# New home addresses for the tiles in SBUF, and down projections that take high and low input parts in one 512-column matmul

## The chip, the cores and the metric

The kernel runs on one core of a Trainium2 chip. The metric is the device time of one execution in microseconds (us), as the median of several runs. The engines are called as the profile calls them: PE (TensorE matmuls), PEld (TensorE weight loads), DVE (VectorE), ACT (ScalarE), POOL (GpSimd) and SP (SyncE, which issues DMAs).

## The reference, cut to what matters

The reference sends 256 tokens of width 1,024 through one block with a mixer (two attentions), a squared-ReLU MLP and a gated per-layer embedding (PLE), and then through two layers of a second block, each with a SwiGLU, a mixer and another SwiGLU. All data are float32.

```python
# first block
x = x + einsum(merged, w_o)                     # mixer
u = relu(einsum(rmsnorm(x, g_mlp), w_up))       # 1024 -> 4096
x = x + einsum(u * u, w_down)                   # 4096 -> 1024
x = x + sigmoid(einsum(rmsnorm(x, g_ple), w_ple_gate)) * einsum(p, w_ple)
# second block, twice
x = x + 0.5 * swiglu(rmsnorm(x, g[0]), ffn_w_in[0], ffn_w_out[0])   # 1024 -> 2 * 2816, 2816 -> 1024
x = x + mixer(rmsnorm(x, g[1]))                 # GLA and forgetting attention, then sparse attention
x = x + 0.5 * swiglu(rmsnorm(x, g[2]), ffn_w_in[1], ffn_w_out[1])
```

## The kernel before

**Layout.** Activations lie with features on the 128 partitions and the 256 tokens along the free dimension: a tile `[128, 8, 256]` is the whole residual `x`. Weights come in one long stream of DMAs of 512 KB, in the order in which they are used (class `Stream`). Each such chunk of 128x1024 lands in `wraw`, ACT casts it to `whi` (the high part, type float32r), and DVE subtracts to get `wlo`, the low part (lines 140 and 149). There are five `wraw`, five `whi` and four `wlo` buffers, of 4,096 bytes a partition each.

**Matmuls.** Every input of a projection is also kept as a high and a low part (`hx` and `lx` for the normalised residual, `gh` and `gl` for the hidden layer, `oh` and `ol` for attention outputs, `mh` and `ml` for the merged mixer). One product of a 128x128 weight piece with a 128x256 input takes three matmuls, with the weights stationary (helper `mm3`, lines 313 to 315):

```python
PE.matmul(o, ah, bh, start=start, stop=False, ...)   # L313: whi x hx
PE.matmul(o, ah, bl, start=False, stop=False, ...)   # L314: whi x lx
PE.matmul(o, al, bh, start=False, stop=stop_, ...)   # L315: wlo x hx
```

Each of the three loads its own 128x128 weights. `gemm_a` walks the output tiles of 128 features in pairs that share one PSUM bank (`acc`, three buffers), and inside a tile over the K inputs. `gemm_b` does the opposite for values and for the last projection: the input is stationary and the weights move, in 256 or 512 columns (lines 363 to 365).

**The stages around the change.** The stages follow each other in program order: mixer, MLP up, MLP down (`w_down`: 8 output tiles, K = 32), PLE, and four SwiGLUs called ffn00, ffn01, ffn10 and ffn11 with a mixer after ffn00 and after ffn10. The down projections of ffn00, ffn01 and ffn10 have 8 output tiles and K = 22; that of ffn11 goes through `gemm_b`. At the end of each pair of output tiles, `ev_down` (L935) or `ev` (L1078) scales the bank by a row, adds it to `x` (L462), and `feed` makes the next stage's `hx` and `lx` (L390, L391) and the squares for its norm (L453, L456, L457). The next stage begins with `lead=6`: two pairs of output tiles take inputs 0 to 5 first, so that inputs 6 and 7 are wanted last. The order of the work on each engine is the order in which the program emits it (a hand-written scheduler, `Sched`).

**Addresses.** A pool lays out its tiles one after the other in each partition, and pools follow each other: constants, `raw`, `hl` (`whi` and `wlo`), `act` (`x`, `hx`, `lx` of 8,192 bytes each, then two `ssq` of 2,048), `tmp` (buffers of 2,048 and 1,024 bytes), `tiny` (7 names of 6 buffers of 64 bytes, 2,688 bytes in all), and then the pool of the current phase. A second stack grows from the top downwards: `pe` with `pt_`, `ph` and `pl`, and under it `hx2` and `lx2`, the inputs of ffn00. A piece of weights starts at a multiple of 512 bytes in its buffer, save in the few chunks that hold a narrow piece, and an input k starts at a multiple of 1,024 bytes in its tile. The pool `raw` starts at byte 21,248, which is 83 times 256.

Of the kernel before, what the change touches and what calls it, by code (L numbers as in the profile page):

```python
# [104 lines left out]
class Stream:  # L105
# [112 lines left out]
def build(ctx, tc, nc, aps, total, stop=None):  # L218
# [3 lines left out]
    raw_pool = pool("raw", RB)  # L222
    hi_pool = pool("hl", HB)
# [19 lines left out]
    hx = act.tile([P, KD, T], F32R, name="hx")  # L243
    lx = act.tile([P, KD, T], F32R, name="lx")
# [67 lines left out]
    def mm3(o, ah, al, bh, bl, start, stop_, joint=False):  # L312
        PE.matmul(o, ah, bh, start=start, stop=False, skip_group_check=joint)  # L313
        PE.matmul(o, ah, bl, start=False, stop=False, skip_group_check=joint)  # L314
        PE.matmul(o, al, bh, start=False, stop=stop_, skip_group_check=joint)  # L315
# [66 lines left out]
    def rhs_of(h, l):  # L382
        return lambda k: (h[:, k], l[:, k])
# [80 lines left out]
    hrhs = rhs_of(hx, lx)  # L464
# [11 lines left out]
    def idx(a, n):  # L476
        return list(range(a, a + n))
# [39 lines left out]
    oh = mpo.tile([P, 8, T], F32R, name="oh")  # L517
    ol = mpo.tile([P, 8, T], F32R, name="ol")
# [34 lines left out]
    ckh = mp.tile([P, T], F32R, name="ckh")  # L553
    ckl = mp.tile([P, T], F32R, name="ckl")
    cqh = mp.tile([P, 2, T], F32R, name="cqh")
    cql = mp.tile([P, 2, T], F32R, name="cql")
# [23 lines left out]
    def ckv_side(c, sq):  # L580
# [12 lines left out]
        split(ckh, ckl, cn)  # L593
# [30 lines left out]
    def tok_scale(ms, n, out, const):  # L624
        """out = tok * rsqrt(tok^2 * ms + eps) * const for ms [P, 2, n]"""
# [248 lines left out]
    mh = mp.tile([P, 8, T], F32R, name="mh")  # L874
    ml = mp.tile([P, 8, T], F32R, name="ml")

    def gemm_merge():
        for i in range(4):
            pss = []
            for wn, k0 in (("w_oa", 0), ("w_ob", 4)):  # L880
                ps = accb()
                pss.append(ps)
                for j in range(2):
                    for k in range(4):
                        wh, wl = W.get((wn, k, idx((2 * i + j) * 128, 128)), P)
                        mm3(ps[:, j * T:(j + 1) * T], wh, wl, oh[:, k0 + k], ol[:, k0 + k], k == 0, k == 3)
# [16 lines left out]
    sc.run(gemm_a(8, 8, sq_cols("w_o"), rhs_of(mh, ml), lambda i, ps: sc.push(lambda: ev_wo(i, ps)), lead=6))  # L903
# [21 lines left out]
    ph = mpp.tile([P, 2, T], F32R, name="ph")  # L925
    pl = mpp.tile([P, 2, T], F32R, name="pl")
# [104 lines left out]
    sc.run(gemm_a(8, 2, sq_cols("w_ple"), rhs_of(ph, pl), ev_ple))  # L1031
# [5 lines left out]
    def ffn(layer, j, rhs, nrm, nxt):  # L1037
        mx, mp = phase("ffn%d%d" % (layer, j))
        gh = mp.tile([P, 22, T], F32R, name="gh")
        gl = mp.tile([P, 22, T], F32R, name="gl")  # L1040
# [30 lines left out]
        if nxt is None:  # L1071
            final(wout, rhs_of(gh, gl), nrm, tok, gfin, xg)
# [161 lines left out]
    def even(nrm, nxt):  # L1234
# [29 lines left out]
        oh = mp.tile([P, 8, T], F32R, name="oh2")  # L1264
        ol = mp.tile([P, 8, T], F32R, name="ol2")
# [228 lines left out]
        sc.run(gemm_a(8, 8, sq_cols("even_w_out"), rhs_of(oh, ol), lambda i, ps: sc.push(lambda: ev_o(i, ps)), lead=(4, 6),  # L1494
# [4 lines left out]
    def odd(nrm, nxt):  # L1499
# [11 lines left out]
        ch = mp.tile([P, 2, T], F32R, name="ch")  # L1511
        cl = mp.tile([P, 2, T], F32R, name="cl")
# [6 lines left out]
        oh = mp.tile([P, 8, T], F32R, name="oh3")  # L1519
        ol = mp.tile([P, 8, T], F32R, name="ol3")  # L1520
# [113 lines left out]
        crhs = rhs_of(ch, cl)  # L1634
# [52 lines left out]
        sc.run(gemm_a(8, 8, sq_cols("odd_w_out"), rhs_of(oh, ol), lambda i, ps: sc.push(lambda: ev_o(i, ps)), lead=4, width=3,  # L1687
# [8 lines left out]
    ffn(0, 0, rhs_of(hx2, lx2), n4, r5)  # L1696
# [96 lines left out]
```

## Time and profile before

| what | value |
|---|---|
| time, median of 3 runs | 1421.72 us (1413.07 to 1423.33) |
| span of the profiled execution, first to last instruction | 1410.7 us |
| PE busy, share of the span | 99% |
| PEld busy | 96% |
| DVE busy, ACT busy | 64%, 49% |
| moved from and to memory, mean | 173 GB/s |

The profile has one execution. Of its own time the profile gives the span; the median of the runs is 11.0 us above the span, the fastest run 2.4 us. Busy time of PE overstates it: a matmul of 256 columns is shown with 280 ns, while the next one starts 0.12 us after it. What a stage costs is therefore read from how many matmuls start in a stretch.

### The profile page before, as it was taken

What the parts mean: (1) busy time and instruction counts of PE and PEld (TensorE: products, weight loads), DVE (VectorE), ACT (ScalarE), POOL (GpSimd) and SP (SyncE); (2) the same over time, 40 slices, a digit from 0 to 9 for tenths busy, and PEclk for the clock granted to TensorE, in tenths of its full rate; (3) what the DMA queues carried; (4) which work ended last, traced back from release to release, by engine and by line L of the source; (5) the groups of instructions that cost most, each with busy time, mean ns of one, the idle gap of its engine ahead of it and who ended that gap; (6) DMA issues with size and microseconds to landing.
All of it is one profiled execution on the core that took longest, in us unless ns stands there. A gap on an engine that the chain in (4) does not pass through costs nothing.

```text
span 1410.7 us, 27027 instructions
## 1 busy us (share of the span) xinstructions
PE 1395.5 (99%) x11278; PEld 1360.4 (96%) x11278; DVE 903.1 (64%) x1241; ACT 685.2 (49%) x959; POOL 102.9 (7%) x108
## 2 busy tenths in 40 slices
PE   8999999999999999999999999999999999999998
PEld 8799999999999999997999999999999988999987
DVE  6766776655577656575765555655555776776553
ACT  6554465544554444453454444444444454644442
POOL 2300000000050000010000000000000171000001
PEclk9999999999999999999999999999999999999999
DMA  8633555555556565653455555555655632555652
GB/s 274 208 102 107 184 191 186 182 189 182 180 165 200 188 184 176 197 168 104 131 183 180 179 180 190 185 184 186 183 182 188 199 120 66 182 190 191 182 177 82
DMA packets 69641, 243.59 MB, mean 173 GB/s; under 512 B 7877, under 2 KB 11365, under 8 KB 69392
## 3 DMA queue, kind: packets, MB, share of 16 engines
q1 hardware_dynamic: 66096, 234.52, 52.2%
q10 hardware_dynamic: 2992, 5.99, 1.3%
q8 instruction: 88, 1.44, 0.4%
q0 software_dynamic: 432, 1.37, 0.3%
q14 instruction: 33, 0.27, 0.1%
HBM read 240.78 MB, written 4.22 MB: 174 GB/s over the span
## 4 chain that ended last, share of the span: by engine, by line
PE 95%; DVE 2%; ACT 1%; POOL 1%; issue 0%; DMA 0%; SPq 0%; POOLq 0%; DVEq 0%; ACTq 0%
PE acc L313 27%; PE acc L314 27%; PE acc L315 27%; PE acc L363 2%; PE acc L365 2%; PE acc L364 2%; PE pv L791 1%; DVE iacc L1588 1%; PE wk L760 1%; PE wk L1181 1%; PE wk L779 0%; PE wk L1660 0%; POOL rs_y L395 0%; PE wk L757 0%; PE wk L1659 0%
## 5 line engine op out<-in xcount | busy, mean ns | idle before, releaser
L149 DVE TENSOR_TENSOR wlo<-wraw,whi 128x1024 fp32r<-128x1024 f32 (+2 forms) x442 | 535.3, 1219 | 274.5 <-PE acc L315 213.0
L140 ACT CAST whi<-wraw 128x1024 fp32r<-128x1024 f32 (+1 forms) x448 | 463.5, 1039 | 396.5 <-PE acc L314 292.3
L313 PE MATMUL acc<-hx,whi 128*128 128x256 f32 x2184 | 629.1, 288 | 1.0 <-ACT whi L140 0.6
L314 PE MATMUL acc<-lx,whi 128*128 128x256 f32 x2184 | 617.1, 283 | 1.4 <-DVE lx L391 1.4
L315 PE MATMUL acc<-hx,wlo 128*128 128x256 f32 x2184 | 617.2, 283 | 0.5 <-DVE wlo L149 0.5
L313 PEld LDWEIGHTS acc<-hx,whi 128*128 128x128 f32 x2184 | 417.0, 191 | 8.3 <-issue 6.3
L314 PEld LDWEIGHTS acc<-lx,whi 128*128 128x128 f32 x2184 | 417.1, 191 | 1.9 <-DVE lx L391 1.6
L315 PEld LDWEIGHTS acc<-hx,wlo 128*128 128x128 f32 x2184 | 416.8, 191 | 0.9 <-DVE wlo L149 0.9
L314 PE MATMUL acc<-gl,whi 128*128 128x256 f32 x784 | 220.7, 281 | 0.0
L313 PE MATMUL acc<-gh,whi 128*128 128x256 f32 x784 | 220.7, 281 | 0.0
L315 PE MATMUL acc<-gh,wlo 128*128 128x256 f32 x784 | 220.7, 281 | 0.0
L313 PEld LDWEIGHTS acc<-gh,whi 128*128 128x128 f32 x784 | 147.6, 188 | 0.0
L314 PEld LDWEIGHTS acc<-gl,whi 128*128 128x128 f32 x784 | 147.6, 188 | 0.0
L315 PEld LDWEIGHTS acc<-gh,wlo 128*128 128x128 f32 x784 | 147.6, 188 | 0.0
L395 POOL TENSOR_TENSOR rs_y<-col,mhalf 128x2 f32<-128x2 f32 (+2 forms) x17 | 19.1, 1125 | 812.3 <-DVE col L423 747.9
L387 DVE TENSOR_TENSOR gl<-t,gh 128x512 fp32r<-128x512 f32 x60 | 41.6, 693 | 41.3 <-ACT gh L386 41.3
L386 ACT CAST gh<-t 128x512 fp32r<-128x512 f32 x60 | 37.2, 621 | 45.7 <-DVE t L1059 33.3
L390 ACT ACTIVATE hx<-x,gains 128x256 fp32r<-128x256 f32 x64 | 29.5, 502 | 56.9 <-DVE x L462 50.0
L313 PE MATMUL acc<-oh,whi 128*128 128x256 f32 x192 | 54.8, 286 | 0.0
L315 PE MATMUL acc<-oh,wlo 128*128 128x256 f32 x192 | 53.7, 280 | 0.0
L314 PE MATMUL acc<-ol,whi 128*128 128x256 f32 x192 | 53.7, 279 | 0.0
L1059 DVE TENSOR_TENSOR t<-t,acc 128x512 f32<-128x512 f32 x44 | 30.3, 688 | 32.4 <-ACT t L1057 32.4
(367 smaller groups left out, 1449.4 us busy)
## 6 DMA issues: line engine op xcount, KB each, us to landing
wraw<-w SPq DMA_DIRECT2D x439, 512.0 KB, 4.1
t5r<-t5u ACTq DMA_DIRECT2D x1, 3072.0 KB, 13.4
Bt<-t5r ACTq DMA_DIRECT2D x1, 2048.0 KB, 10.9
wraw<-w SPq DMA_DIRECT2D x7, 256.0 KB, 5.2
x<-xt SPq DMA_DIRECT2D x8, 128.0 KB, 4.9
rope<-cst SPq DMA_DIRECT2D x1, 640.0 KB, 7.7
gfin<-gfin POOLq DMA_DIRECT2D x1, 512.0 KB, 4.9
out<-xg ACTq DMA_DIRECT2D x2, 256.0 KB, 2.8
```

Of the source, the lines that this page charges most:

```text
L140: self.nc.scalar.copy(self.hi[c][:, :n], self.raw[c][:, :n])
L149: self.low_eng.tensor_tensor(self.lo[c][:, :n], self.raw[c][:, :n], self.hi[c][:, :n].bitcast(F32), op=OP.subtract)
L313: PE.matmul(o, ah, bh, start=start, stop=False, skip_group_check=joint)
L314: PE.matmul(o, ah, bl, start=False, stop=False, skip_group_check=joint)
L315: PE.matmul(o, al, bh, start=False, stop=stop_, skip_group_check=joint)
L363: PE.matmul(o[b][:, :N], xh[:, s], w[0], start=(k == 0), stop=False)
L364: PE.matmul(o[b][:, :N], xl[:, s], w[0], start=False, stop=False)
L365: PE.matmul(o[b][:, :N], xh[:, s], w[1], start=False, stop=(k == K - 1))
L386: S_.copy(hi, src)
L387: V.tensor_tensor(lo, src, hi.bitcast(F32), op=OP.subtract)
L390: S_.activation(hi, src, AF.Copy, scale=g)
L1059: V.tensor_tensor(u, s, ps, op=OP.mult)
```

## The change

Tiles move to other addresses, the two parts of every input come to lie side by side in one tile, and the down projections of the MLP, ffn00, ffn01 and ffn10 use a new loop.

- Unused pad tiles are laid between the pools: 64 bytes ahead of `hl`, 192 behind it, 128 behind `tiny`, 192 behind `oh` in the first mixer, 224 in the pool `pe`.
- `halves_of` makes one tile with the high part of input k, then its low part, then input k+1. `past` leaves out some 4-byte elements at its start: 32 for the MLP, and for the SwiGLUs 4 * j, with 60 more where the layer's number is above j (0 for ffn00, 4 for ffn01, 60 for ffn10, 4 for ffn11).
- `gemm_w` takes one bank for each output tile: one matmul of 512 columns through `whi` (high and low part of the input, into the two halves of the bank), one of 256 columns through `wlo` into the first half.
- `add_row` empties a bank: ACT copies the second half out, DVE adds the first half to it, scales, and adds to `x`. It runs for each tile and not for each pair; the squares are still made for each pair.

```diff
+    pad(pool("p0"), 64)
     hi_pool = pool("hl", HB)
+    pad(pool("p1"), 192)
     act = pool("act")
     tmp = pool("tmp", 3)
     tiny = pool("tiny", 6)
+    pad(pool("p2"), 128)
...
+    def halves_of(p, n, name, past=0):
+        t = p.tile([P, n * 2 * T + past], F32R, name=name)[:, past:].rearrange("p (n h t) -> p n h t", n=n, h=2)
+        return t, t[:, :, 0], t[:, :, 1]
+    xx, hx, lx = halves_of(act, KD, "hx")
...
+    def gemm_w(n, K, piece, rhs, done):
+        for t in range(n):
+            ps = accb()
+            for k in range(K):
+                wh, wl = W.get(piece(t, k), P)
+                PE.matmul(ps, wh, rhs(k), start=(k == 0), stop=False, skip_group_check=True)
+                PE.matmul(ps[:, :T], wl, rhs(k)[:, 0], start=False, stop=(k == K - 1), skip_group_check=True)
+                yield
+            done(t, ps)
...
-    oh = mpo.tile([P, 8, T], F32R, name="oh")
-    ol = mpo.tile([P, 8, T], F32R, name="ol")
+    oo, oh, ol = halves_of(mpo, 8, "oh")
+    pad(mpo, 192)
...
-    gh = mp.tile([P, 32, T], F32R, name="gh")
-    gl = mp.tile([P, 32, T], F32R, name="gl")
+    gg, gh, gl = halves_of(mp, 32, "gh", 32)
...
-    def ev_down(i, ps):
-        t = t512()
-        V.tensor_tensor(v2(t), v2(ps), bc(r2row, 2), op=OP.mult)
-        add_x(i, v2(t))
-        r3.feed(i)
+    def add_row(k, ps, row, nxt, f=1.0):
+        low, t = s256(), s256()
+        S_.copy(low, ps[:, T:])
+        V.tensor_tensor(t, ps[:, :T], low, op=OP.add)
+        V.scalar_tensor_tensor(t, t, f, row, op0=OP.mult, op1=OP.mult)
+        V.tensor_tensor(x[:, k], x[:, k], t, op=OP.add)
+        nxt.part(k)
+        if k % 2:
+            nxt.square(k // 2)
-    sc.run(gemm_a(8, 32, sq_cols("w_down"), rhs_of(gh, gl), lambda i, ps: sc.push(lambda: ev_down(i, ps))))
+    sc.run(gemm_w(8, 32, sq_cols("w_down"), rhs_of(gg), lambda k, ps: sc.push(lambda: add_row(k, ps, r2row, r3))))
...
-        gh = mp.tile([P, 22, T], F32R, name="gh")
-        gl = mp.tile([P, 22, T], F32R, name="gl")
+        gg, gh, gl = halves_of(mp, 22, "gh", 4 * j + 60 * (layer > j))
...
-        sc.run(gemm_a(8, 22, sq_cols(wout), rhs_of(gh, gl), lambda i, ps: sc.push(lambda: ev(i, ps))))
+        sc.run(gemm_w(8, 22, sq_cols(wout), rhs_of(gg), lambda k, ps: sc.push(lambda: add_row(k, ps, nrm.row, nxt, 0.5))))
```

The other tiles with two parts (`hx2`, `mh`, `oh2`, `oh3` and the small latents) are laid out by `halves_of` in the same way, and `oh2` and `oh3` move to the front of their pools. The pool `pe` gets `pad(mpp, 224)`.

## Rows read from the trace of the kernel before

**Rows 1.** The page: busy time, clock in 40 slices, chain that ended last.

```profile
PE 1395.5 (99%) x11278; PEld 1360.4 (96%) x11278; DVE 903.1 (64%) x1241; ACT 685.2 (49%) x959; POOL 102.9 (7%) x108
PEclk9999999999999999999999999999999999999999
PE 95%; DVE 2%; ACT 1%; POOL 1%; issue 0%; DMA 0%; SPq 0%; POOLq 0%; DVEq 0%; ACTq 0%
```

**Rows 2.** Stretches: length, busy (instructions) by engine, clock, DMA share, GB/s.

```profile
core 0: us, PE busy (x) PEld busy (x) DVE busy (x) ACT busy (x) POOL busy (x), PEclk, DMA share, GB/s
166.00:187.00 21.00, 21.00 (x188) 21.00 (x187) 16.93 (x23) 12.83 (x18) 0.00 (x0) 1.00 0.60 197
200.00:270.00 70.00, 70.00 (x586) 70.00 (x585) 46.37 (x50) 39.13 (x49) 0.00 (x0) 1.00 0.56 181
284.00:370.00 86.00, 86.00 (x727) 86.00 (x726) 45.53 (x46) 36.21 (x41) 0.00 (x0) 1.00 0.59 186
443.00:520.00 77.00, 77.00 (x653) 77.00 (x652) 45.62 (x48) 36.50 (x41) 0.00 (x0) 1.00 0.61 191
```

**Rows 3.** Other stretches, PE alone: length, busy (matmuls), clock, DMA share, GB/s.

```profile
144.00:165.00 21.00, 21.00 (x179) 1.00 0.54 173
692.00:712.00 20.00, 20.00 (x173) 1.00 0.50 172
914.00:1026.00 112.00, 112.00 (x935) 1.00 0.59 180
1198.00:1213.00 15.00, 15.00 (x135) 1.00 0.50 162
1346.00:1370.00 24.00, 24.00 (x105) 1.00 0.61 197
```

**Rows 4.** Groups by line and shape: count, busy us, mean ns, idle before.

```profile
L313 PE MATMUL acc<-hx,whi 128*128 128x256 f32 x2176 | 626.9, 288 | 1.0 <-ACT whi L140 0.6 <-ACT hx L390 0.4
L315 PE MATMUL acc<-gh,wlo 128*128 128x256 f32 x784 | 220.7, 281 | 0.0
L313 PE MATMUL acc<-oh,whi 128*128 128x256 f32 x192 | 54.8, 286 | 0.0
L363 PE MATMUL acc<-whi,gh 128*128 128x256 f32 x88 | 24.9, 283 | 0.0
L313 PE MATMUL acc<-mh,whi 128*128 128x256 f32 x64 | 17.7, 276 | 0.0
L363 PE MATMUL acc<-whi,gh 128*128 128x512 f32 x44 | 17.4, 396 | 0.0
```

**Rows 5.** Who waited for whom: total us, times, longest us.

```profile
ACT whi L140 <- PE acc L314: 292.3, 160, 4.8
DVE wlo L149 <- PE acc L315: 213.0, 133, 2.0
```

**Rows 6.** Order of time on DVE around the end of ffn00: start, us, instruction.

```profile
590.08 0.69 DVE L1078 SCALAR_TENSOR_TENSOR t<-acc,row 128x512 f32<-128x512 f32 x1
590.80 0.69 DVE L462 TENSOR_TENSOR x<-x,t 128x512 f32<-128x512 f32 x1
592.07 0.89 DVE L391 SCALAR_TENSOR_TENSOR lx<-x,gains,hx 128x256 fp32r<-128x256 f32 x2 [0.58 <-ACT hx L390]
593.72 0.42 DVE L415 TENSOR_TENSOR ssq<-ssq 128x256 f32<-128x256 f32 x1
599.77 0.42 DVE L1444 SCALAR_TENSOR_TENSOR qf<-acc,row 128x256 f32<-128x256 f32 x1 [0.78 <-ACT row L429]
```

**Rows 7.** The same stretch on ACT.

```profile
591.53 0.51 ACT L390 ACTIVATE hx<-x,gains 128x256 fp32r<-128x256 f32 x1 [1.95 <-DVE x L462]
599.37 0.37 ACT L429 COPY row<-wk 128x256 f32<-128x256 f32 x1 [0.68 <-PE wk L404]
```

More of the change, by code (lines that the diff above doesn't have):

```diff
@@ L222, in build, with pad @@
     raw_pool = pool("raw", RB)
+    def pad(p, n):
+        p.tile([P, n // 4], F32, name="pad_%d" % len(pads))
+        pads.append(n)
+    pads = []
+    pad(pool("p0"), 64)
     hi_pool = pool("hl", HB)
+    pad(pool("p1"), 192)
     act = pool("act")
@@ L310, in bc, with mm3 @@
         return ap[:, None, :].to_broadcast([ap.shape[0], n, ap.shape[1]])
[L312 to L315, printed above, removed]
+    def mm3(o, ah, al, b, start, stop_, joint=False):
+        PE.matmul(o, ah, b[:, 0], start=start, stop=False, skip_group_check=joint)
+        PE.matmul(o, ah, b[:, 1], start=False, stop=False, skip_group_check=joint)
+        PE.matmul(o, al, b[:, 0], start=False, stop=stop_, skip_group_check=joint)
+    def gemm_w(n, K, piece, rhs, done):
[7 more added lines that the diff above has]
+            done(t, ps)
     def gemm_a(n, K, piece, rhs, done, M=P, lead=0, width=2, order=None, ready=None, joint=False):
@@ L328, in part @@
                 wh, wl = W.get(piece(t, k), m)
-                xh, xl = rhs(k)
-                mm3(ps[:m, j * T:(j + 1) * T], wh, wl, xh, xl, k == order[0] and not (joint and j), k == order[-1], joint)
+                mm3(ps[:m, j * T:(j + 1) * T], wh, wl, rhs(k), k == order[0] and not (joint and j), k == order[-1], joint)
                 yield
@@ L380, in gemm_b, with rhs_of @@
             done(o)
[L382 to L383 removed]
+    def rhs_of(t):
+        return lambda k: t[:, k]
     def split(hi, lo, src):
@@ L552, in build @@
     vB = mp.tile([P, 2, P], F32, name="vB")
[L553 to L556, printed above, removed]
+    ck, ckh, ckl = halves_of(mp, 1, "ckh")
+    cq, cqh, cql = halves_of(mp, 2, "cqh")
     fA = mp.tile([P, 2], F32, name="fA")
@@ L852, in latents @@
     def latents():
-        yield from gemm_a(4, 1, lambda t, k: ("w_kvb", 0, idx(t * 256, 64) + idx(t * 256 + 128, 64)), lambda k: (ckh, ckl), ev_kn)
+        yield from gemm_a(4, 1, lambda t, k: ("w_kvb", 0, idx(t * 256, 64) + idx(t * 256 + 128, 64)), rhs_of(ck), ev_kn)
         yield from gemm_b(512, 1, lambda k: ("w_kvb", 0, [h * 128 + 64 + j for h in range(8) for j in range(64)]),
-                          lambda k: (ckh, ckl), lambda p: sc.push(lambda: ev_va(p)))
-        yield from gemm_a(8, 2, lambda t, k: ("w_qb", k, qa_cols(t)), rhs_of(cqh, cql), ev_qa)
+                          rhs_of(ck), lambda p: sc.push(lambda: ev_va(p)))
+        yield from gemm_a(8, 2, lambda t, k: ("w_qb", k, qa_cols(t)), rhs_of(cq), ev_qa)
     def ev_gate(i, ps):
@@ L873, in build @@
     mx, mp = phase("mx1b")
-    mh = mp.tile([P, 8, T], F32R, name="mh")
-    ml = mp.tile([P, 8, T], F32R, name="ml")
+    mm, mh, ml = halves_of(mp, 8, "mh")
     def gemm_merge():
@@ L901, in ev_wo @@
         r2.feed(i)
-    sc.run(gemm_a(8, 8, sq_cols("w_o"), rhs_of(mh, ml), lambda i, ps: sc.push(lambda: ev_wo(i, ps)), lead=6))
+    sc.run(gemm_a(8, 8, sq_cols("w_o"), rhs_of(mm), lambda i, ps: sc.push(lambda: ev_wo(i, ps)), lead=6))
     close(mx)
@@ L924, in build @@
     pt_ = mpp.tile([P, 2, T], F32, name="pt_")
-    ph = mpp.tile([P, 2, T], F32R, name="ph")
-    pl = mpp.tile([P, 2, T], F32R, name="pl")
+    pp, ph, pl = halves_of(mpp, 2, "ph")
+    pad(mpp, 224)
     G.dma_start(pt_, aps["pt"])
@@ L945, in build @@
     mxo, mpo = phase("hx2", "right")
-    hx2 = mpo.tile([P, KD, T], F32R, name="hx2")
-    lx2 = mpo.tile([P, KD, T], F32R, name="lx2")
+    xx2, hx2, lx2 = halves_of(mpo, KD, "hx2")
     gfg = cpool.tile([P, 8], F32, name="gfg")
@@ L1029, in ev_ple @@
         S_.activation(pe[:, 2 * i:2 * i + 2], v2(ps), AF.Copy, scale=0.5)
-    sc.run(gemm_a(8, 2, sq_cols("w_ple"), rhs_of(ph, pl), ev_ple))
+    sc.run(gemm_a(8, 2, sq_cols("w_ple"), rhs_of(pp), ev_ple))
     sc.run(gemm_a(8, 8, sq_cols("w_ple_gate"), hrhs, lambda i, ps: sc.push(lambda: ev_pg(i, ps), lambda: r3.norm.ready)))
@@ L1241, in even @@
             c0 += w
+        oo, oh, ol = halves_of(mp, 8, "oh2")
         wg = mp.tile([16, T], F32, name="wg")
@@ L1263, in even @@
         Bia = mp.tile([P, 8, 3, P], F32, name="Bia")
-        oh = mp.tile([P, 8, T], F32R, name="oh2")
-        ol = mp.tile([P, 8, T], F32R, name="ol2")
         Fs = mp.tile([P, 16], F32, name="Fs")
@@ L1492, in ev_o @@
             nxt.feed(i)
-        sc.run(gemm_a(8, 8, sq_cols("even_w_out"), rhs_of(oh, ol), lambda i, ps: sc.push(lambda: ev_o(i, ps)), lead=(4, 6),
+        sc.run(gemm_a(8, 8, sq_cols("even_w_out"), rhs_of(oo), lambda i, ps: sc.push(lambda: ev_o(i, ps)), lead=(4, 6),
                       width=3, order=[4, 5, 6, 7, 0, 1, 2, 3], ready=lambda k: has("fox" if k > 3 else "gla%d" % (k // 2))))
@@ L1505, in odd @@
             c0 += w
+        oo, oh, ol = halves_of(mp, 8, "oh3")
         Bt = mp.tile([P, 16, T], F32, name="Bt")
@@ L1510, in odd @@
         vh = mp.tile([P, 2, 1024], F32, name="vh")
-        ch = mp.tile([P, 2, T], F32R, name="ch")
-        cl = mp.tile([P, 2, T], F32R, name="cl")
+        cc_, ch, cl = halves_of(mp, 2, "ch")
         ki = [mp.tile([P, T], F32, name="ki%d" % j) for j in range(2)]
@@ L1685, in ev_o @@
             nxt.feed(i)
-        sc.run(gemm_a(8, 8, sq_cols("odd_w_out"), rhs_of(oh, ol), lambda i, ps: sc.push(lambda: ev_o(i, ps)), lead=4, width=3,
+        sc.run(gemm_a(8, 8, sq_cols("odd_w_out"), rhs_of(oo), lambda i, ps: sc.push(lambda: ev_o(i, ps)), lead=4, width=3,
                       ready=lambda k: has(k // 4), joint=True))
@@ L1695, in build @@
     r5 = g2(0, 1)
-    ffn(0, 0, rhs_of(hx2, lx2), n4, r5)
+    ffn(0, 0, rhs_of(xx2), n4, r5)
     close(mxo)
```

21 lines of the change are left out of this document (6 added, 15 removed).

## The prediction

> **What bounds the kernel now.** I read the page first: PE is busy all the time, its clock is granted in full in every slice, and the chain that ended last lies on PE for 95% of the span [rows 1]. So the price of a matmul decides. Busy time doesn't give that price, because matmuls overlap; the count in a stretch does. A matmul lasts 0.28 us and one starts every 0.12 us, so a stretch also counts 2.4 that began before it. The price is then the length divided by (count - 2.4).
>
> The stretches of one kind of work [rows 2, 3] give for 256 columns:
>
> | stretch | moving tile | ns per matmul |
> |---|---|---|
> | 166 to 187 | mh, ml | 21,000 / 185.6 = 113.1 |
> | 1198 to 1213 | oh3, ol3 | 113.1 |
> | 200 to 270; 914 to 1026 | hx, lx | 119.9; 120.1 |
> | 284 to 370 | gh, gl of the MLP | 118.7 |
> | 443 to 520 | hx2, lx2 | 118.4 |
> | 144 to 165 | oh, ol, first mixer | 118.9 |
> | 692 to 712 | oh2, ol2 | 117.2 |
>
> All have clock 1.00 and the same shape, and in every one PE and PEld are busy without a hole. Late weights aren't the reason either: ACT and DVE stand waiting for PE to free their buffers (160 and 133 times [rows 5]). What differs is the place in SBUF. I take the gap from the first byte of the weights to the first byte of the moving tile, modulo 256 bytes, from the sizes of the tiles. The buffers of `whi` and `wlo`, `x`, `hx` and `lx` are all multiples of 256, so hx has gap 0. The tiles of `tiny` (2,688 bytes) shift the phase pools by 128: gh and oh have gap 128. In the first mixer `tab` adds 64: mh has gap 192, and so has oh3 (64 bytes of `ws` ahead of it). oh2 has 160, and hx2, laid out from the top, 224. The price goes with the gap: 0 costs 120.0, 128 118.8, 160 117.2, 224 118.4, and 192 costs 113.1, twice, in stages that have nothing else in common. My reading: the weight load for the next matmul and the moving input of this one are read at the same time and get into each other's way, unless the gap is 192.
>
> In sentences by themselves: the Trainium skill, "TensorE: Matmul & The Clock Gate", section "Step-by-step: what each phase is for", says that PE has two independent read ports, one for the moving operand and one for the weights. By that the gap would be worth nothing, which is rival A below; the 113.1 beside 120.0 of the rows speaks against it.
>
> **The change part by part.**
>
> *Homes.* The first pad puts the weights 64 bytes on, the second (64 + 192 = 256) leaves hx where it was, the third makes the phase pools start at 128 + 256 + 128, a multiple of 256. With 192 bytes ahead of `tab`, mh starts at 0, and the 224 on the top stack bring hx2 to 0. All moving tiles of `gemm_a` are then at 0 and the weights at 64: gap -64, that is 192, the one that costs 113.1. mh and oh3 keep it. High and low part side by side are 1,024 bytes apart and change no gap.
> - hx: 3 x 2,176 matmuls [rows 4], of which ffn00 has 44 x 8 x 3 = 1,056 on hx2; of the other 5,472 I leave out some 200 that stand singly between attention instructions. 5,270 x (120.0 - 113.1) = 36.4 us.
> - hx2: 1,056 x 5.3 = 5.6 us.
> - oh: 192 x 5.8 = 1.1; oh2: 192 x 4.1 = 0.8; the small latents and ph, under 100, 0.5. Together 2.4 us.
>
> *Down projections.* 784 triples (8 x 32 + 3 x 8 x 22, the count of L315 [rows 4]) cost 3 x 118.7 = 356.1 ns each now. Each becomes one matmul of 512 columns and one of 256, so two weight loads in place of three and the same 768 columns. No such pair is in this trace, but 512 columns are: in ffn11's `gemm_b` one lasts 0.395 us, and 24,000 / (105 - 1.7) = 232.3 ns are between two [rows 3] at gap 128. Twice 113.1 is 226.2, and 232.3 is 6.1 above, much what one load costs too much at that gap with 256 columns (5.7). So I take the 6.4 ns over 256 columns at 2.4 GHz (106.7) as a cost of columns, not of instructions, and 226.2 + 113.1 = 339.3 ns for a pair whose loads collide with nothing, plus the collisions of two loads:
> - MLP: `past` adds 128 bytes, gap 64. No row has it; its neighbours 0 and 128 cost 6.9 and 5.7, I take 6.3. 351.9 ns, gain 256 x 4.2 = 1.1 us.
> - ffn00: gap 192, 339.3 ns, gain 176 x 16.8 = 3.0 us.
> - ffn01: 16 bytes more, gap 208, halfway between 192 (nothing) and 224 (5.3): 344.6 ns, 176 x 11.5 = 2.0 us.
> - ffn10: 240 bytes more, gap 176, halfway between 160 (4.1) and 192: 343.4 ns, 176 x 12.7 = 2.2 us.
>
> Sum 8.3 us. Its ends: every load at the worst gap, 353.1 ns and 2.4 us; none colliding, 13.2 us; and, if the 6.4 ns were paid once for each instruction, 219.7 + 113.1 = 332.8 ns and 18.3 us.
>
> *ffn11's down projection.* Its weights move and gg, 16 bytes on, is stationary: gap 48, taken like its neighbours 0 and 128, no change. There are 3 x (88 + 44) = 396 loads at 5.7 to 6.1 ns each [rows 4], so between 0.5 us lost and 2.3 us gained.
>
> *Emptying a bank.* For each pair of tiles ACT gets two copies of 0.37 [rows 7] more, and DVE six operations of 0.42 in place of two of 0.69 [rows 6], 1.1 us. The MLP's four pairs take 91 us, in which DVE is busy for 53% and ACT for 42% [rows 2]; this is hidden. Without that cover it would cost (0.74 + 1.1) x 16 = 29 us. Behind the last tile, what counts is when lx for k = 7 is there. Before: from 590.08 (bank read) to 592.96 (second lx), 2.9 us [rows 6, 7]. After: copy 0.37, three operations of 0.42, hx 0.51, lx 0.45, 2.6 us, with the hand-overs about 2.9. The next stage wants input 6 after 36 matmuls, 4.3 us now and 4.1 after. The cover holds with over 1 us. The weight casts queued behind it on ACT and DVE move little.
>
> *What is given back.* In the 5% of the chain that isn't PE, some 70 us, matmuls are cover for attention and norm chains, and faster ones end in a longer wait: 70 / 0.12 = 580 matmuls x 6.9 = 4.0 us less.
>
> *Sum.* 36.4 + 5.6 + 2.4 + 8.3 + 0 - 4.0 = 48.7 us. The span would be 1410.7 - 48.7 = 1362.0, and with the 11.0 us by which the median lies above the span, 1373.
>
> **The rivals.**
>
> *A. The homes are worth nothing*, because the gap isn't the cause, or because pads that nobody uses get no room and the tiles stay where they are. Then only the loop counts: 232.3 + 118.7 = 351.0 for 356.1, 784 x 5.1 = 4.0 us, 1418. For it: the stretches at 113.1 are only two and short. Against it: no third thing that they share shows in the rows.
>
> *B. The place itself counts, not the gap* (slower). If a moving tile that starts at a multiple of 256 costs 120.0 wherever the weights are, then hx stays, mh and oh3 lose 384 x 6.9 = 2.6 us, hx2 1,056 x 1.6 = 1.7, oh and oh2 192 x (1.1 + 2.8) = 0.7; the MLP's pairs gain 256 x 5.1 = 1.3, and the 528 others cost 360 for 356.1, 2.1 us. Together 5.8 us slower, 1428. It decides from the point where hx at 0 stays at 120 with the weights at 64. Against it: with weights moving and gh stationary, places exchanged, a matmul of 256 columns is still shown with 283 ns, as gh's 281 and not hx's 288 [rows 4].
>
> *C. Something else takes over halfway.* A chunk of eight pieces is eaten in 24 x 113.1 = 2.71 us in place of 2.88. If the casts, the DMAs or the DVE work of the stages held it to about the middle, half of the gain is left: 1397. For it: DVE is at 66% and DMA at 0.56 in the hx stretches. Against it: mh's stretch runs at 113.1 with DVE at 81%, 197 GB/s and no hole [rows 2].
>
> **How the numbers follow.** The forecast, 1373, gets 0.76; A 0.07, B 0.06, C 0.11. The range: below, the best end of the down projections (10.0 more), of ffn11 (2.3) and nothing given back (4.0) make 1357, and as the fastest run shown lies 8.6 us under the median I go to 1354. Above it takes in C, to 1400. That leaves out A and B. A measurement of this kernel can tell about 1% from no change (its three runs lie 0.7% apart). Faster by over 1%: the forecast and C, 0.86; within 1%: A and most of B, 0.12; slower by over 1%: 0.02.
>
> **What would show it.** In the profile after: stretches of hx at 113 ns per matmul in place of 120, with counts up by 6%; hx2 and oh at 113 too; mh and oh3 as before. In the down projections 339 ns for a pair in ffn00, more in the MLP; a PE without holes at the starts of the stages behind them. If hx still starts every 120 ns, the reading of the gap is wrong (A or B); if holes stand ahead of L313 with ACT or DVE as releaser, it is C; a pair under 335 ns would show that the cost beyond columns is one of instructions.

## The result and the profile after

The changed kernel takes 1396.76 us (median of 4 runs, 1391.53 to 1398.3), beside 1417.56 us of the kernel before in the same session: a ratio of 0.985 with the 95% interval 0.981 to 0.989. The span of the profiled execution fell from 1410.7 to 1389.8 us, by 20.9 us where 48.7 were forecast. The time lies inside the range and the sign is right, but 27.8 us of the forecast gain are missing, so the sum has a wrong term.

The page of the kernel after (span, first and third line of busy times and clock), which answers to [rows 1]:

```profile
span 1389.8 us, 25505 instructions
PE 1371.9 (99%) x10494; PEld 1301.1 (94%) x10494; DVE 919.6 (66%) x1305; ACT 695.3 (50%) x991; POOL 100.9 (7%) x108
PEclk9999999999999999999999999999999999999999
```

PE is still busy all the time, with 784 matmuls less, one for each pair of the new loop, and the clock is still granted in full. So again only the price of a matmul can have moved. Stretches of the kernel after, PE alone, which answer to the stretches of [rows 2, 3] (length, busy and matmuls of PE, clock, DMA share, GB/s):

```profile
145.00:185.00 40.00, 40.00 (x355) 1.00 0.57 190
200.00:270.00 70.00, 70.00 (x597) 1.00 0.57 190
284.00:355.00 71.00, 71.00 (x404) 1.00 0.57 187
425.00:515.00 90.00, 90.00 (x767) 1.00 0.58 190
527.00:577.00 50.00, 50.00 (x285) 1.00 0.57 184
690.00:704.00 14.00, 14.00 (x121) 1.00 0.63 218
720.00:818.00 98.00, 98.00 (x867) 1.00 0.61 193
830.00:885.00 55.00, 55.00 (x314) 1.00 0.54 182
905.00:1005.00 100.00, 100.00 (x851) 1.00 0.59 190
1020.00:1070.00 50.00, 50.00 (x288) 1.00 0.58 191
1180.00:1194.00 14.00, 14.00 (x121) 1.00 0.52 183
```

Read as before, length / (count - 2.4), and for the down projections 2 x length / (count - 1.9) for a pair:

| stretch | work | gap | ns before | ns after | forecast |
|---|---|---|---|---|---|
| 145 to 185 | oh and mh, first mixer | 192 | 118.9, 113.1 | 113.4 | 113.1 |
| 200 to 270 | hx, MLP up | 192 | 119.9 | 117.7 | 113.1 |
| 425 to 515 | hx2, ffn00 up | 192 | 118.4 | 117.7 | 113.1 |
| 690 to 704 | oh2 | 192 | 117.2 | 118.0 | 113.1 |
| 720 to 818 | hx, ffn01 up | 192 | 119.9 | 113.3 | 113.1 |
| 905 to 1005 | hx, ffn10 up | 192 | 120.1 | 117.8 | 113.1 |
| 1180 to 1194 | oh3 | 192 | 113.1 | 118.0 | 113.1 |
| 284 to 355 | pairs, MLP | 64 | 356.1 | 353.1 | 351.9 |
| 527 to 577 | pairs, ffn00 | 192 | 356.1 | 353.2 | 339.3 |
| 830 to 885 | pairs, ffn01 | 208 | 356.1 | 352.4 | 344.6 |
| 1020 to 1070 | pairs, ffn10 | 176 | 356.1 | 349.5 | 343.4 |

One matmul more or less in a count moves a price of this table by 0.1 to 0.8%; from start to start in the trace, the pairs of the four stages cost 353.3, 353.3, 353.3 and 350.0, for 356.0 of a triple before.

hx still starts at a multiple of 256 bytes and no longer costs 120, as it would by the prediction's rival B. But the moving tiles of 256 columns now all have the same gap and don't have the same price: there are two, 113.3 and 117.7 ns. ffn01 and ffn10 run the same loop over the same tiles, one at each price, and oh3, which kept its gap, became dearer. The timeline of PE shows where the price changes (start and duration in us, engine, line, operation, tile, shapes, number):

```profile
187.90 0.28 PE L332 MATMUL acc<-hx,wlo 128*128 128x256 f32 x1
188.01 0.28 PE L330 MATMUL acc<-hx,whi 128*128 128x256 f32 x1
...
188.36 0.50 PE L440 MATMUL wk<-cst_sb,ssq 128*128 128x1 f32 x4
...
189.86 0.28 PE L330 MATMUL acc<-hx,whi 128*128 128x256 f32 x1
189.98 0.28 PE L331 MATMUL acc<-hx,whi 128*128 128x256 f32 x1
...
689.58 0.30 PE L331 MATMUL acc<-oh,whi 128*128 128x256 f32 x1
689.72 0.28 PE L332 MATMUL acc<-oh,wlo 128*128 128x256 f32 x1
...
714.66 0.38 PE L432 MATMUL wk<-cst_sb,rs_y 128*128 128x128 f32 x2
```

Ahead of the norm's four single-column matmuls at 188.36 three starts take 0.34 us; ten matmuls behind them, from 189.86 on, they are 0.12 us apart and three take 0.35 to 0.36, and it stays so through the whole stage. At 689.58 one matmul took 0.14 us to the next start instead of 0.11, and all of oh2 behind it runs at 118. At 714.66 two transposes bring the price from 118 back to 113, and all of ffn01 up has it. So the price at gap 192 has a state, which a small disturbance can flip and which then lasts. Not every one does: the same two groups at the start of ffn10's up projection, at 894.3 and 897.5 us, leave it at 118. Counted by starts six matmuls long, some 2,000 of about 7,400 matmuls at this gap ran at the cheap price and some 4,700 at the dear one; the others stand among other instructions.

By kinds of work, with the mean times between starts of both traces, the 20.9 us are: hx 5,285 x (119.8 - 116.5) = 17.4; hx2 0.8; oh 1.0; oh2 0.15; oh3 -0.7; the pairs 784 x 3.4 = 2.7; ffn11's down projection 0.5; 21.9 together. The 1.0 by which this exceeds the 20.9 is covered by waits that grew: those that the profile lists for PE add up to 10.5 us for 8.2 before, and two of 1.1 us each are new, L440 for `ssq` and L432 for `col`, around the norm that ends the first block.

### The profile page after: what moved, and what is told of

Read it like the earlier page. It is cut to its first block, busy times and chain, and to the rows that moved or that the text cites. A ratio compares the mean times of both kernels' runs of the same rounds, so it can differ in the third digit from the quotient of the medians.

```text
span 1389.8 us, 25505 instructions
## 1 busy us (share of the span) xinstructions
PE 1371.9 (99%) x10494; PEld 1301.1 (94%) x10494; DVE 919.6 (66%) x1305; ACT 695.3 (50%) x991; POOL 100.9 (7%) x108
## 4 chain that ended last, share of the span: by engine, by line
PE 69%; DVE 1%; POOL 0%; ACT 0%; issue 0%; POOLq 0%; DVEq 0%; ACTq 0%
PE acc L330 15%; PE acc L332 15%; PE acc L331 15%; PE acc L341 9%; PE acc L342 4%; PE acc L391 2%; PE acc L392 2%; PE acc L393 2%; PE wk L1202 1%; PE wk L1678 0%; PE wk L1677 0%; DVE iacc L1606 0%; PE pv L1214 0%; PE pv L1215 0%; PE pv L1213 0%; PE wk L440 0%
## 5 line engine op out<-in xcount | busy, mean ns | idle before, releaser
L149 DVE TENSOR_TENSOR wlo<-wraw,whi 128x1024 fp32r<-128x1024 f32 (+2 forms) x442 | 532.9, 1221 | 213.3 <-PE acc L332 106.3
L330 PE MATMUL acc<-hx,whi 128*128 128x256 f32 x2184 | 623.5, 285 | 0.8 <-ACT whi L140 0.8
L331 PE MATMUL acc<-hx,whi 128*128 128x256 f32 x2184 | 611.7, 280 | 1.4 <-DVE hx L419 1.4
L330 PEld LDWEIGHTS acc<-hx,whi 128*128 128x128 f32 x2184 | 410.2, 188 | 7.9 <-issue 6.3
L331 PEld LDWEIGHTS acc<-hx,whi 128*128 128x128 f32 x2184 | 412.8, 189 | 2.4 <-DVE hx L419 2.0
L341 PE MATMUL acc<-gh,whi 128*128 128x512 f32 x784 | 276.6, 396 | 0.0
L415 DVE TENSOR_TENSOR gh<-t,gh 128x512 fp32r<-128x512 f32 x60 | 41.6, 693 | 41.3 <-ACT gh L414 41.3
L330 PE MATMUL acc<-oh,whi 128*128 128x256 f32 x192 | 54.7, 285 | 0.0
L331 PE MATMUL acc<-oh,whi 128*128 128x256 f32 x192 | 53.6, 279 | 0.0
L419 DVE SCALAR_TENSOR_TENSOR hx<-x,gains,hx 128x256 fp32r<-128x256 f32 x64 | 31.7, 512 | 29.9 <-ACT hx L418 29.9
L1084 ACT ACTIVATE t<-t 128x512 f32<-128x512 f32 x44 | 27.8, 632 | 44.4 <-DVE t L1082 44.3
## 6 DMA issues: line engine op xcount, KB each, us to landing
t5r<-t5u ACTq DMA_DIRECT2D x1, 3072.0 KB, 13.3
```

The lines of the kernel that those rows point to most:

```text
L149: self.low_eng.tensor_tensor(self.lo[c][:, :n], self.raw[c][:, :n], self.hi[c][:, :n].bitcast(F32), op=OP.subtract)
L330: PE.matmul(o, ah, b[:, 0], start=start, stop=False, skip_group_check=joint)
L331: PE.matmul(o, ah, b[:, 1], start=False, stop=False, skip_group_check=joint)
L341: PE.matmul(ps, wh, rhs(k), start=(k == 0), stop=False, skip_group_check=True)
L415: V.tensor_tensor(lo, src, hi.bitcast(F32), op=OP.subtract)
L419: V.scalar_tensor_tensor(lo, src, g, hi.bitcast(F32), op0=OP.mult, op1=OP.subtract)
```

## The experiments

**The theory** behind them: the gap (first byte of the moving tile less first byte of the weights, modulo 256) sets the price, but at 192 two prices are possible, and disturbances choose. **Its rivals**: at gap 192 the price is 113 and other engines' traffic or late work in the stage raises it to 118; the place of the moving tile alone counts; the new down loop, and not the homes, brings the gain.

### e1_homes_only: the homes, with the old down projections

```diff
-    sc.run(gemm_w(8, 32, sq_cols("w_down"), ...))
+    sc.run(gemm_a(8, 32, sq_cols("w_down"), rhs_of(gg), lambda i, ps: sc.push(lambda: ev_down(i, ps))))
...
-        sc.run(gemm_w(8, 22, sq_cols(wout), ...))
+        sc.run(gemm_a(8, 22, sq_cols(wout), rhs_of(gg), lambda i, ps: sc.push(lambda: ev(i, ps))))
```

> All new homes, but the down projections keep the old three matmuls of 256 columns and the emptying by pairs. Theory P (the price of a matmul depends on the gap and on a phase between the weight load and the moving input, which some disturbance sets and which then stays; at gap 192 there are two prices, near 113 and near 118 ns): most of the gain is the homes', ratio to the kernel before 0.983 to 0.989, the triples of the down projections at 113 to 118.7 ns per matmul. Rival L (the gain of the whole change comes from the loop of 512 columns): ratio 0.995 to 1.00. Rival S (what the other engines do in a stage sets the price): the same stages as in the changed kernel are at 113 and the same at 118.

Measured: 1393.77 us, ratio 0.988 (0.983 to 0.992), span 1391.3. Its stretches of hx in the MLP, gh in the MLP and hx in ffn01:

```profile
200.00:270.00 70.00, 70.00 (x596) 1.00 0.59 189
284.00:355.00 71.00, 71.00 (x605) 1.00 0.58 187
720.00:818.00 98.00, 98.00 (x867) 1.00 0.61 194
```

These are 117.9, 117.8 and 113.3 ns: the same stages are cheap and dear as in the kernel after, without the new loop. That the same stages are dear is also what the rival of the other engines says; e1 doesn't part it from the theory. A triple at gap 64 costs 353.4 ns, as much as the pair there (353.3 from start to start); in ffn01 and ffn10, at gaps 208 and 176, triples cost 357.5 and 357.8, more than the 356.0 before and above what was expected. The gain of the whole change is that of the homes. By starts the pairs of the kernel after take 276.4 us and the triples here 278.5, so the loop is worth 2.1; the times of the two kernels (medians 1396.76 and 1393.77, spans 1389.8 and 1391.3) don't show it.

### e2_no_pads: the new loop and parts side by side, without pads

```diff
-    pad(pool("p0"), 64)
-    pad(pool("p1"), 192)
-    pad(pool("p2"), 128)
-    pad(mpo, 192)
-    pad(mpp, 224)
-    gg, gh, gl = halves_of(mp, 32, "gh", 32)
+    gg, gh, gl = halves_of(mp, 32, "gh")
-        gg, gh, gl = halves_of(mp, 22, "gh", 4 * j + 60 * (layer > j))
+        gg, gh, gl = halves_of(mp, 22, "gh")
```

> The new loop with parts side by side, but no pads, so that hx stays at gap 0 and the hidden layers at 128 as in the kernel before (oh3 goes from gap 192 to 128). Theory P: hx at 120 ns, pairs at 232 + 119 = 351 ns for 356, less about 1 us for oh3, 3 us gained, ratio 0.996 to 1.000. Rival L: ratio 0.985 to 0.990. Rival B of the prediction (the place counts, not the gap) says the same as P here.

Measured: 1412.05 us, ratio 0.998 (0.996 to 0.999), span 1410.5, for 1410.7 before. hx in the MLP and pairs in the MLP:

```profile
200.00:270.00 70.00, 70.00 (x586) 1.00 0.57 187
290.00:350.00 60.00, 60.00 (x344) 1.00 0.56 186
```

hx is back at 119.9 ns, with the very count of [rows 2]. The pair at gap 128 costs 350.8 (351.0 from start to start, 230.5 + 120.5), which is what rival A's 232.3 + 118.7 gave. So without the pads the change is worth next to nothing, and two weight loads in place of three save 5 ns of 356, not 17.

### e3_gap_sweep: all gaps in multiples of 16, PE alone

A kernel with nothing but streams of 16 triples, and then of 16 pairs, four streams at each gap; weights stay where they are and the moving tile is shifted. Between streams stands a group of small fp32 matmuls, by turns single columns and 128 columns.

```python
for fn in (triples, pairs):
    for g in range(0, 256, 16):
        for r in range(4):
            o = fn(g, 16)            # moving input at weights + g bytes
            (stat, trans)[r % 2]()   # small fp32 matmuls
```

> Leaves out the whole model: PE alone, streams of 16 triples (256 columns) and then of 16 pairs (512 and 256 columns) at each gap from 0 to 240 bytes in steps of 16, four streams for each gap, with a small float32 matmul group between them; the other engines are idle. Theory P: gap 0 always near 120 ns; at 192 streams near 113 and streams near 118 both occur, each constant within its stream; pairs lie between 339 and 353 ns and some gap is better than those of the changed kernel. Rival S: with the other engines idle each gap has one price, and 192 has 113 in every stream.

Measured, ns from start to start in the four streams of a gap, once the price of a stream has settled:

| gap | matmul of 256 columns | pair | gap | matmul of 256 columns | pair |
|---|---|---|---|---|---|
| 0 | 120.0 | 346.5 | 128 | 118.6 to 118.8 | 350.6 to 351.8 |
| 16 | 118.7 or 113.3 | 346.5, one 360 | 144 | 118.7 | 346.5 |
| 32 | 116.7 to 117.8 | 346.5 | 160 | 117.4 or 118.8 | 346.5 |
| 48 | 118.4 | 346.7 or 349.9 | 176 | 119.2 | 350.0 |
| 64 | 117.8 | 349.0 or 352.7 | 192 | 117.8, 113.3, 117.8, 113.3 | 353.4 |
| 80 | 118.2 to 120.0 | 353.4 | 208 | 119.0 | 350.2 or 353.6 |
| 96 | 120.0 | 350 | 224 | 118.3 | 346.6 or 353 |
| 112 | 113.3 to 113.7 | 353.3 | 240 | 117.1 | 353 |

Stretches inside one stream at gap 96, two at 112 and four at 192:

```profile
168.90:173.90 5.00, 5.00 (x44) 1.00 0.01 3
...
193.70:198.70 5.00, 5.00 (x46) 1.00 0.00 0
199.70:204.70 5.00, 5.00 (x46) 1.00 0.02 3
315.70:320.70 5.00, 5.00 (x45) 1.00 0.00 0
321.70:326.70 5.00, 5.00 (x47) 1.00 0.01 3
327.70:332.70 5.00, 5.00 (x45) 1.00 0.00 0
333.70:338.70 5.00, 5.00 (x47) 1.00 0.02 3
```

That is 44 matmuls in 5 us at gap 96, 46 at 112, and 45, 47, 45, 47 at 192. With PE alone gap 192 takes two prices by turns, so other engines aren't needed for it. Gap 112 is cheap in every stream. For the pairs the best homes are others (0, 32, 144, 160), and 192, which ffn00 got, is among the worst: 353.4, as in the kernel after.

### e4_modes: gap 192 alone, with ACT and DVE idle and busy

Three sections of 24 streams: weights at 64 and moving tile at 0; the same with a cast on ACT and a subtraction on DVE running all along; weights at 0 and moving tile at 192.

```python
section(64, 0)
section(64, 0, True)   # with S_.copy(hi, ra) and V.tensor_tensor(lo, ra, hi, op=OP.subtract)
section(0, 192)
```

> Leaves out the whole model: three sections of 24 streams of 16 triples at gap 192, a small float32 matmul group ahead of each stream. Section 1: weights at 64, moving tile at 0, other engines idle. Section 2: the same with casts on ACT and subtractions on DVE running beside it all the time. Section 3: weights at 0, moving tile at 192, idle. Theory P: both prices, near 113 and near 118 ns, in all three sections, and no more of the dear ones in section 2. Rival S: section 2 dear, sections 1 and 3 at 113. Rival B (place): section 3 at 113, section 1 at 118.

Measured, from start to start: in all three sections 113.3 and 117.8 ns alternate from stream to stream, after the first two. Two streams that follow each other in the second section, all engines (PE, PEld, DVE, ACT, POOL):

```profile
188.60:193.60 5.00, 5.00 (x46) 5.00 (x45) 5.00 (x5) 4.53 (x5) 0.00 (x0) 1.00 0.00 0
194.50:199.50 5.00, 5.00 (x45) 5.00 (x44) 5.00 (x6) 4.45 (x5) 0.00 (x0) 1.00 0.01 3
```

DVE and ACT are busy in both and the price differs; in the quiet sections it differs in the same way. That ends the rival of the other engines. It also ends rival B: with the gap kept, moving both places by 64 bytes changes nothing.

### e5_gap112: every moving tile at gap 112, old down projections

```diff
-    pad(pool("p0"), 64)
+    pad(pool("p0"), 160)
-    pad(pool("p1"), 192)
+    pad(pool("p1"), 96)
-    pad(pool("p2"), 128)
+    pad(pool("p2"), 96)
-    def halves_of(p, n, name, past=0):
+    def halves_of(p, n, name, past=4):
...
-    sc.run(gemm_w(8, 32, ...))
+    sc.run(gemm_a(8, 32, ...))   # as in e1_homes_only, for the SwiGLUs too
```

Some further pads and values of `past` (160, 192 and 224 bytes; 60, and 12 in ffn11) bring the tiles of the other pools to the same gap.

> Old loop of three matmuls, parts side by side, every moving tile at gap 112 (pads of 160, 96 and 96 bytes, tiles 16 bytes on; in the last down projection the moving weights at 112 from the hidden layer). Theory P, with the prices of the gap sweep (113.3 to 113.7 ns in all four streams at 112): every stage near 113.5 ns whatever happened before it; 5,285 hx x 6.3 + 1,050 hx2 x 4.8 + 2,352 gh x 5.2 + some 3 us, less 4 us given back, 50 us, ratio 0.963 to 0.970. Rival S (the price comes from what else runs in the stage): no better than the homes-only run, ratio 0.984 to 0.992. Rival C of the prediction (casts, DMAs or the emptying of banks hold PE back once matmuls are cheap): matmuls at 113.5 but holes, ratio 0.975 to 0.985.

Measured: 1370.35 us, ratio 0.968 (0.965 to 0.970), span 1368.5. It is the fastest of all kernels here, 42.2 us under the span before and 21.3 under that of the change. hx, gh, hx2, then hx of ffn01 and ffn11:

```profile
200.00:265.00 65.00, 65.00 (x576) 1.00 0.64 198
280.00:350.00 70.00, 70.00 (x620) 1.00 0.64 196
420.00:500.00 80.00, 80.00 (x709) 1.00 0.63 202
715.00:815.00 100.00, 100.00 (x885) 1.00 0.61 195
...
1200.00:1300.00 100.00, 100.00 (x879) 1.00 0.62 198
```

113.3, 113.3, 113.2, 113.3 and 114.1 ns, and 113.3 in ffn10 as well: the forecast price, in all stages, at the same clock of 1.00. The stretches have no hole, so rival C falls too: DMA, casts and DVE keep up. The waits show what is given back; of this kernel, and behind it the same wait in the kernel after (in all, times, longest):

```profile
PE acc L391 <- DVE q L1651: 3.5, 1, 3.5
```

```profile
PE acc L391 <- DVE q L1638: 1.3, 1, 1.3
```

PE waits 2.2 us longer for the sparse attention's chain on DVE in the third mixer, and its listed waits are 13.3 us in all, for 8.2 in the kernel before. By starts the kinds of work of e5 are worth 50.6 us (hx 5,285 x 5.9 = 31.2, hx2 1,050 x 4.9 = 5.1, gh 784 x 16.0 = 12.5, oh and oh2 1.8), and 42.2 of span came. So 8.4 are given back, twice the 4.0 that the forecast, and this run's expectation, allowed for; 5.1 of them are seen as waits.

### e6_gap96: all of e5_gap112, 16 bytes earlier

```diff
-        t = p.tile([P, n * 2 * T + past], F32R, name=name)[:, past:].rearrange(...)
+        t = p.tile([P, n * 2 * T + past], F32R, name=name)[:, past - 4:past - 4 + n * 2 * T].rearrange(...)
```

> As the run at gap 112, with every moving tile 16 bytes earlier in the same tile, gap 96. Theory P, with the gap sweep (119.9 to 120.1 ns in all four streams at 96): hx stays at 120, hx2 and gh get 1.3 ns dearer; 1,050 x 1.6 + 2,352 x 1.3 + oh, mh and oh3 some 4 us, 8 us slower than the kernel before, ratio 1.003 to 1.009. If the layout side by side or the pads as such were what helps: ratio as at gap 112.

Measured: 1423.06 us, ratio 1.005 (1.003 to 1.007). hx and gh:

```profile
200.00:265.00 65.00, 65.00 (x544) 1.00 0.58 180
285.00:355.00 70.00, 70.00 (x585) 1.00 0.57 181
```

120.0 and 120.2 ns. Same instructions, order and sizes of tiles, 16 bytes: 54.2 us of span. In sentences by themselves: the Trainium skill ("TensorE: Matmul & The Clock Gate", "Step-by-step: what each phase is for") says that PE reads the moving operand and the weights through two independent ports, and that loading the next weights takes no read bandwidth from the running matmul. By that alone these two kernels would be equal; 113.3 beside 120.0 decides against it here.

### e7_gap112_pairs160: e5_gap112 with the 512-column loop at one of its best gaps

```diff
-    sc.run(gemm_a(8, 32, ...))
+    sc.run(gemm_w(8, 32, ...))   # gap 160 by past = 16; the SwiGLUs in the same way
```

> As the run at gap 112, but the down projections of the MLP, ffn00, ffn01 and ffn10 go through the new loop with their hidden layer at gap 160, the best gap of pairs in the sweep (346.5 ns in all four streams). Theory P: 346.5 ns for a pair, 784 x (346.5 - 340.2) = 5 us slower than the run at gap 112, ratio 0.966 to 0.974: the loop is worth less than a good home. If fewer weight loads are worth something in themselves: faster than the run at gap 112.

Measured: 1376.37 us, ratio 0.973 (0.970 to 0.976), span 1374.3. Pairs in the MLP:

```profile
275.00:340.00 65.00, 65.00 (x377) 1.00 0.61 192
```

2 x 65,000 / (377 - 1.9) = 346.6 ns, 229.2 + 117.5, as the sweep said; three matmuls at 113.3 are 339.9. The loop loses 5.8 us of span to the old one, 784 x 6.7 = 5.3 from this row. With each at its best home among the multiples of 16, one instruction less costs time.

### e8_kicks: small matmuls put into the changed kernel

```diff
+    def kicks():
+        yield 40
+        for i in range(8):
+            ps = wk()
+            for b in range(2):
+                if i % 2:
+                    PE.matmul(ps[:, b:b + 1], C("one"), onecol(D), start=True, stop=True)    # L951
+                else:
+                    PE.transpose(ps[:, b * P:(b + 1) * P], C("one"), ident)                  # L953
+            yield 24
+    sc.side(kicks())                                                                         # in the MLP's up projection
```

> The changed kernel (gap 192) with eight small float32 matmul groups put into the MLP's up projection, one every 24 triples, by turns two transposes and two single-column matmuls whose results nobody uses. Theory P: between these the price is constant, and it jumps between 117.8 and 113.3 ns at some of them, so that a part of the stage runs at 113; the eight cost some 0.3 us each. Rival S: 117.8 from end to end, as in the changed kernel.

Measured: 1398.58 us in one run. One of the groups in the timeline, and the stretches between the groups:

```profile
208.44 0.50 PE L951 MATMUL wk<-cst_sb 128*128 128x1 f32 x4
```

```profile
199.80:208.30 8.50, 8.50 (x74) 1.00 0.63 187
209.80:217.00 7.20, 7.20 (x66) 1.00 0.66 205
218.60:225.60 7.00, 7.00 (x62) 1.00 0.50 162
227.00:233.80 6.80, 6.80 (x62) 1.00 0.61 190
```

118.7, 113.2, 117.4, 114.1, and 117.9 behind the next group: behind every group of single columns 113 to 114, behind every pair of transposes 117 to 119, and from the last group (260.5) to the end of the stage 113. The new price sets in five to eight matmuls behind the single columns, and at once behind the transposes. So the state can be switched on purpose, inside the real kernel, with all other work unchanged. The stages behind show it too; the up projections of ffn00 and of ffn01, further on in the same trace:

```profile
425.00:515.00 90.00, 90.00 (x797) 1.00 0.63 199
720.00:825.00 105.00, 105.00 (x894) 1.00 0.59 185
```

These are 113.3 and 117.8 ns, for 117.7 and 113.3 in the kernel after: the two stages have changed prices, though nothing in them was edited. No gain shows in the whole time of this one run.

### e9_columns: what a matmul costs beyond its columns

Streams of 24 matmuls of one size, each with its own weight load, at all gaps in multiples of 16, PE alone.

```python
for n in (128, 256, 384, 512):
    for g in range(0, 256, 16):
        for r in range(2):
            o = same(n, g, 24)
            (stat, trans)[r % 2]()
```

> Leaves out the whole model: PE alone, streams of 24 matmuls of one size (128, 256, 384, then 512 columns), each with its own weight load, two streams at each gap in steps of 16 bytes. The forecast took 226.2 ns for 512 columns without a collision, twice 113.1. Theory columns (what lies over N / 2.4 GHz grows with the columns): at the best gap 56.6, 113.1, 169.7 and 226.2 ns. Rival instructions (6.4 ns for each matmul): 59.7, 113.1, 166.4 and 219.7 ns, and then no pair need cost over 333 ns at its best gap.

Measured, best gap: 111.5 to 111.9 ns for 128 columns at every gap, 113.3 for 256, 173.3 for 384, 226.7 for 512 (at gap 0; 228.9 to 236.9 at the others). Over the columns at 2.4 GHz, the level granted here (53.3, 106.7, 160.0, 213.3), the last three lie 6.7, 13.3 and 13.3 ns. The forecast's cost by columns would be 6.4, 9.6 and 12.8, one by instructions 6.4 for all: neither fits. 226.7 is close to the forecast's 226.2, but at another gap than 192. With 128 columns the time hardly depends on the gap. In sentences by themselves: the Trainium skill ("TensorE: Matmul & The Clock Gate", "LDWEIGHTS (loading the stationary operand)") gives about P / 1.2 ns for a load of P columns, by which 128 columns are an estimated 106.7 ns. The 111.6 here lies 5 ns above it, so the load may set the pace of these streams; no run here shows that it does.

### e10_fine_sweep: gaps in multiples of 4 bytes

As e3_gap_sweep, with 10 triples in a stream and steps of 4 bytes.

> Leaves out the whole model: PE alone, streams of 10 triples at each gap from 0 to 252 bytes in steps of 4, four streams for each gap. Theory P as it now stands (the gap decides which prices are open, the phase which of them is taken): 113.3 to 113.7 in all four streams in a band around 112 that is narrower than 32 bytes (96 has 120, 128 has 118.7); around 16 and 192 bands in which 113 and 118 both occur. If the 113 at 112 came from the order of the streams and not from the gap, other gaps than those show 113, and 112 doesn't in all four.

Measured: gap 112 alone is cheap in all four streams (113.3 to 114.7 ns). 108 has 120.0 and 116 has 121.7; 192 changes between 113.3 and 117.8; 16 reached 113.3 once. All others lie between 116.6 and 124.4, the worst being 132. The home is exact to 4 bytes, narrower than the band that I had expected, and around 16 and 192 there is no band either: 188 has 118.2 and more, 196 has 121.9 and more.

## Why the prediction was half right

- **What bounds the kernel**: right. PE stays busy at clock 1.00 in every kernel here, and the spans follow from prices between starts: the terms of the kernel after add up to its 20.9 us within 1.0.
- **The reading of the gap**: the step that failed. It says that moving input and weight load get into each other's way "unless the gap is 192". The gap does decide (e5 and e6 differ by 16 bytes and 54.2 us; place and other engines don't matter in e4), but at 192 there are two prices, 113.3 and 117.8, and a state that small disturbances can flip (e3, e4, e8). Both stretches that showed 113.1 in [rows 2, 3] were in the cheap state. Two short stretches that agree were taken as the price of the gap; one of them, oh3, costs 118.0 in the kernel after without having changed its gap. That the two reads collide is still only a reading: the runs show that the gap sets the price, not by what.
- **The terms of the homes** fell with it: hx 17.4 us instead of 36.4, hx2 0.8 instead of 5.6, oh, oh2 and oh3 together 0.5 instead of 1.9 (2.4 with the small latents). Of the 27.8 us that are missing, 19.0 are hx's and 4.8 hx2's. At a gap with one price (e5) the stretches of hx and hx2 reach the forecast 113, so the size of these terms was right for a home that really is cheap.
- **The down projections**: 2.7 us instead of 8.3, a second term that was mis-sized. The pair's uncollided price of 339.3 was carried over from matmuls of 256 columns at 192. Pairs have their own dependence on the gap (e3), in which 192 is among the worst and no multiple of 16 is under 346. The lower end given, 353.1 and 2.4 us, is about what came. The base, 351.0 at gap 128, was exact (e2), and that row alone would have priced the loop well.
- **ffn11's down projection**: 0.5 us, inside the bounds given.
- **Emptying a bank** is hidden, as forecast. The tail of ffn00 in the kernel after, ACT and DVE in the order of time, which answers to [rows 6, 7]:

```profile
583.96 0.37 ACT L960 COPY s<-acc 128x256 f32<-128x256 f32 x1 [0.44 <-PE acc L342]
585.75 0.51 ACT L418 ACTIVATE hx<-x,gains 128x256 fp32r<-128x256 f32 x1 [1.41 <-DVE x L963]
```

```profile
584.37 0.42 DVE L961 TENSOR_TENSOR s<-acc,s 128x256 f32<-128x256 f32 x1 [0.54 <-ACT s L960]
584.83 0.43 DVE L962 SCALAR_TENSOR_TENSOR s<-s,row 128x256 f32<-128x256 f32 x1
585.29 0.42 DVE L963 TENSOR_TENSOR x<-x,s 128x256 f32<-128x256 f32 x1
586.29 0.48 DVE L419 SCALAR_TENSOR_TENSOR hx<-x,gains,hx 128x256 fp32r<-128x256 f32 x1 [0.58 <-ACT hx L418]
```

  From the bank's copy at 583.96 to the end of the low part at 586.77 are 2.8 us, for 2.9 forecast, and PE has no hole at the start of the next stage.
- **Given back**: 1.0 us in the kernel after, as the difference between the terms and the span, where 4.0 were forecast for a much larger gain. Where nearly that gain came, in e5, it is 8.4: the term was too small by half, and the small gain hid it.
- **Rivals**: A fell (e1 gains from homes alone), B fell (e4), C fell: the time it gave, 1397, is what was measured, but its mechanism isn't there, so that it came out right by luck. No stretch has a hole, and with the same DMA, casts and DVE work e5 runs at 113.3.

Open: what makes a gap cheap, why the state lasts, and what decides which way a group flips it. In e3 and e4 the same two kinds of group stand ahead of opposite prices, and so they do in the kernel after and in e8, so the kind alone doesn't tell. Each kernel was traced in one execution; that a stage takes the same state in every execution isn't shown.

## What to carry to other kernels

Where PE is the bound, read the price of a matmul from counts in stretches, stage by stage, and where equal shapes differ, sweep the address of the moving tile against the weights in a small kernel before laying out pools; here 16 bytes were worth 3.8%. A price seen in one or two short stretches may be one state of two: look for the same gap at another price, and for the instruction at which it changes. Fewer instructions need not be cheaper: compare each form at its own best home.

## What the runs showed of the hardware that was not expected

- With float32r inputs of 256 columns and a weight load for each matmul, the time between starts runs from 113.3 to 124.4 ns by the gap alone; of all multiples of 4 bytes only 112 was cheap in every stream (e10).
- At gap 192 the price is 113.3 or 117.8 and holds for whole stages of about 100 us. It changed behind four single-column matmuls and behind two transposes, in either direction, and once at one matmul that came 22 ns late; at other groups of the same kinds it stayed.
- The best price for 384 and 512 columns lies 13.3 ns over the columns' own time, for 256 columns 6.7; and the gaps that are best differ: 112 for 256 columns, 0 for 512.
